# The sums of two weight quarters: GpSimd or VectorE, in an encoder layer with Winograd-like products

## The chip, the cores and the metric

The kernel runs on one core of one Trainium2 chip. The metric is the device time of one execution in microseconds (us); the time before is the median of three runs.

## The reference

One encoder layer on two token sets, 1024 prompt and 512 sample tokens, width 2048, all in fp32. In short:

```
h = rms_norm(x, pre_g);  z = h @ w_in            # 2048 -> 5632 columns
q, k, v, g_attn, u, vg, g_gmlp = split(z)
a = window_attention(rope(q), rope(k), v, sink) * silu(g_attn)
m = spatial_gating(gelu(u), gelu(vg), ln_g, ln_b, ws, bs) * silu(g_gmlp)
y = concatenate([a, m]) @ w_out
x = x + rms_norm(y, post_g)
x = x + sigmoid(x @ w_pg) * (p @ w_pe)
```

The three big products (w_in, w_out, w_pg) are where the change lies.

## The kernel before

**Products.** Each of the big products is cut into 2x2 blocks: two halves of the 1536 tokens (768 each), two halves of the inner dimension (1024 each), and the weight columns in pairs of 128. A pair is computed with seven block products instead of eight, in the manner of Strassen and Winograd: tables A_OF and B_OF (lines 48 to 51) name, for each of the seven, one operand quarter or the sum or difference of two (sign 0, 1 or -1), and one weight quarter or the sum or difference of two. In both tables five of the seven have a sign other than 0. The sums of the products are made when they leave PSUM (leave_product, line 250).

**Sweeps, segments, passes.** There are five sweeps (line 786): a, b and c for w_in, y for w_out, p for w_pg, with 8, 6, 8, 8 and 8 pairs. A sweep runs the seven products in the order 3, 5, 7, 1, 4, 2, 6 (line 46); one product over all pairs of a sweep is a segment, one product of one pair a pass. A pass is 48 matmuls: eight slices k of the inner dimension, two groups of 384 tokens, and three matmuls each, as every operand and weight is split in a high and a low part (mm3, lines 170 to 174).

**Operands and weights.** The operand of a segment, eight tiles of 128x768, is loaded by fetch_operand (line 230), summed on VectorE where the table says so, and split by split_operand (line 244): ScalarE copies the tile into the high part (line 163), VectorE subtracts to get the low part (line 165). There are eight buffers for split operands, so tile k of the next segment can be split only when the last pass of this one has used tile k. The weights of a pass, one tile of 128x1024, are made by make_weights (line 212): it issues the loads of one or two quarters on SyncE, then sums two quarters on GpSimd where the sign isn't 0 (line 223, through add or sub at lines 152 and 155), then splits the sum like an operand (line 227). Raw weight tiles (pool wrp) have four buffers, split ones (wtp) three. The raw tiles stand in the profile as wra, wrb, wrc, wry, wrp by sweep, the split ones as wta to wtp, the operands as ara and aa and so on.

**Order of the work.** The order of each engine's instructions is the order in which the program emits them, and that is planned by the class Line (line 54): every piece of work is a generator, and the number that it yields is the time in us after which its next part is due, on a clock that advances by 0.1733 us a matmul. So the weight job for pass j + 3 is started 1.5 us into pass j (line 873), its sum is due 9.0 us after its loads, its split 3.5 us after the sum, once pass j has been emitted (line 225); the split's subtraction comes 1.2 us behind its copy.

**Beside the products** run the embedding product p @ w_pe at the start (its results leave PSUM by VectorE copies, line 385), the norms, rope (lines 471 to 483, with two steps on GpSimd), the attention and the gating blocks. GpSimd also adds the squares of x for the norm (line 322) and the last sum of the output (line 556).

Of the kernel before, what the change touches and what calls it, by code (L numbers as in the profile page):

```python
# [90 lines left out]
def when(done):  # L91
    while not done():
        yield 0.5
# [3 lines left out]
def tile_encoder_layer(ctx: ExitStack, tc: tile.TileContext, xT, pT, wall, pre_g, post_g, sink,  # L97
# [62 lines left out]
    V, G = nc.vector, nc.gpsimd  # L160

    def split_to(src, hi, lo, us=1.2):
        nc.scalar.activation(hi, src, AF.Copy)  # L163
        yield us
        sub(V, lo, src, hi.bitcast(F32))
# [27 lines left out]
    def load_w(dst, f, h):  # L193

        if f[0] == "c":
            load(dst, wall[f[1], :, h * 1024:(h + 1) * 1024])
            return
        for i in range(2):
            src = wall[f[1] + 2 * h + i].rearrange("p (k n) -> p k n", k=4)
            load(dst[:, i * 512:(i + 1) * 512].rearrange("p (k n) -> p k n", k=4),  # L200
                 src[:, :, f[2]:f[2] + P])
# [10 lines left out]
    def make_weights(j, sw, pr, i):  # L212

        nm = f"{sw.name}{pr}_{i}"
        sign, *quarters = B_OF[pr]
        rs = []
        for kh, n in quarters:
            r = wrp.tile([P, 1024], F32, tag="wr", name=f"wr{nm}_{n}{kh}")
            load_w(r, sw.pairs[i][n][0], kh)
            rs.append(r)  # L220
        yield 9.0
        if sign:
            (add if sign > 0 else sub)(G, rs[0], rs[0], rs[1])
            yield 3.5
        yield from when(lambda: passes[0] >= j - 2)
        w = wtp.tile([P, 2, 1024], F32R, tag="wt", name=f"wt{nm}")
        yield from split_to(rs[0], w[:, 0, :], w[:, 1, :])
        weights[j] = w
# [174 lines left out]
    def embed():  # L403
        for j in range(16):
            line.until(lambda: j // 4 in wpe)
            if j in (1, 6):
                line.spawn(pe_weights(2 + j // 4))
            if j == 8:
                line.spawn(load_late())
            if j == 12:  # L410
                line.spawn(make_weights(1, *items[1]))
            w = wpe[j // 4]
            for h in range(2):
                line.until(lambda: (0, h) in pq and (1, h) in pq)
                ps = banks(f"pspe{j}_{h}")
                for k in range(2):
                    a = (j % 4) * 256 + k * P
                    for c in range(2):
                        mm3(ps[:, c, 0:CH], [w[:, s, a:a + P] for s in range(2)],
                            [pq[k, h][:, s, c * CH:(c + 1) * CH] for s in range(2)], k == 0, k == 1, 0.1733)  # L420
                    line.run_due()
                line.spawn(leave_pe(j, h, ps), 0.1)
# [435 lines left out]
    made_along = {(0, k) for k in range(8)} | {(2, k) for k in range(8)} | {(S_P, k) for k in range(8)}  # L858

    line.spawn(make_weights(0, *items[0]), 34.0)  # L860
    line.spawn(x0_normed(), 25.0)
    embed()
    pq.clear()
    embedded.append(True)
    line.spawn(make_weights(2, *items[2]))

    j = 0
# [99 lines left out]
```

## Time and profile before

| | |
|---|---|
| median of three runs | 2611.05 us (2610.92 to 2614.11) |
| the profiled execution | 2611.79 us |
| its span, first to last instruction | 2610.0 us |
| mean granted TensorE clock | 0.983 |
| busy: PE, DVE, ACT, POOL | 2503.3, 1703.8, 958.4, 736.8 us |
| DMA | 645.97 MB, mean 248 GB/s |

PE is TensorE, DVE VectorE, ACT ScalarE, POOL GpSimd, SP SyncE. A row of the profile names a group of instructions by line, engine, operation and tiles (out<-in, buffer numbers left out); "<-" followed by an engine names what ended a wait. A line such as L152 is that of the helper add, so it is shared by many tiles. Matmuls overlap, so PE counts as busy when it is merely slow; the number of matmuls in a stretch (x290) tells its pace. A DVE instruction is recorded to its end and the next one may start 0.08 us before that.

### The profile page before, as it was taken

Reading aid. Unit: us, or ns where it says so; the run is one execution under the profiler, and the core shown is the slowest. Engines: PE = TensorE matmul, PEld = TensorE weight load, DVE = VectorE, ACT = ScalarE, POOL = GpSimd, SP = SyncE. Lnnn points to the kernel's source line nnn. Section 1 sums busy time; section 2 is a strip of 40 time slices with the busy share of each in tenths; the row PEclk is TensorE's granted clock in tenths of the full one; section 3 lists DMA queues with packets and bytes.
Section 4 is the critical chain, followed back from the end, with each engine's and each line's share of the span. In section 5 each row is a group of like instructions: output and inputs, shape, how many; then the busy total and the mean of one; then the engine's idle time right before and its main releaser. Section 6 shows DMA issues by size and latency. Waiting matters only on the chain.

```text
span 2610.0 us, 36511 instructions
## 1 busy us (share of the span) xinstructions
PE 2503.3 (96%) x14268; PEld 2462.0 (94%) x14268; DVE 1703.8 (65%) x1883; ACT 958.4 (37%) x1378; POOL 736.8 (28%) x316
## 2 busy tenths in 40 slices
PE   5998999999999999999999999999999999999998
PEld 5998999999989999999999999999999999999998
DVE  3657566766667757777767665465566876666773
ACT  3142222323675543333546732332232223322321
POOL 4164324355012202302222013112310321433434
PEclk8999999999999999999999999999999999999999
DMA  6967776666575679879656677566577987879885
GB/s 228 360 237 239 259 248 218 202 206 235 181 263 183 186 245 298 308 252 308 211 173 223 215 269 256 211 224 222 171 233 253 332 302 287 284 246 318 306 301 204
DMA packets 372109, 645.97 MB, mean 248 GB/s; under 512 B 29280, under 2 KB 211680, under 8 KB 371936
## 3 DMA queue, kind: packets, MB, share of 16 engines
q1 hardware_dynamic: 371936, 643.63, 72.7%
q8 instruction: 112, 1.84, 0.3%
q14 instruction: 61, 0.50, 0.1%
HBM read 533.43 MB, written 110.10 MB: 247 GB/s over the span
## 4 chain that ended last, share of the span: by engine, by line
PE 71%; DVE 12%; ACT 5%; issue 5%; POOL 3%; DMA 3%; SPq 0%; POOLq 0%; DVEq 0%; ACTq 0%
PE psy L172 5%; PE psy L173 5%; PE psy L171 5%; PE psp L172 5%; PE psc L173 5%; PE psc L172 5%; PE psp L173 5%; PE psc L171 5%; PE psp L171 5%; PE psa L172 4%; PE psa L171 4%; PE psa L173 4%; PE psb L172 3%; PE psb L173 3%; PE psb L171 3%
## 5 line engine op out<-in xcount | busy, mean ns | idle before, releaser
L171 PE MATMUL psa<-aa,wta 128*128 128x384 f32 x896 | 304.8, 340 | 9.0 <-DVE oa L152 5.2
L172 PE MATMUL psa<-aa,wta 128*128 128x384 f32 x896 | 304.2, 339 | 3.2 <-DVE aa L155 3.2
L171 PE MATMUL psy<-ay,wty 128*128 128x384 f32 x896 | 303.1, 338 | 4.1 <-ACT ay L163 4.1
L171 PE MATMUL psc<-ac,wtc 128*128 128x384 f32 x896 | 305.9, 341 | 1.0 <-ACT ac L163 1.0
L172 PE MATMUL psp<-ap,wtp 128*128 128x384 f32 x896 | 301.6, 337 | 4.6 <-DVE ap L155 4.6
L172 PE MATMUL psy<-ay,wty 128*128 128x384 f32 x896 | 303.1, 338 | 2.2 <-DVE ay L155 2.2
L171 PE MATMUL psp<-ap,wtp 128*128 128x384 f32 x896 | 301.5, 337 | 3.8 <-ACT ap L163 3.8
L172 PE MATMUL psc<-ac,wtc 128*128 128x384 f32 x896 | 301.5, 337 | 1.7 <-DVE ac L155 1.7
L173 PE MATMUL psa<-aa,wta 128*128 128x384 f32 x896 | 303.0, 338 | 0.0
L173 PE MATMUL psy<-ay,wty 128*128 128x384 f32 x896 | 302.3, 337 | 0.0
L173 PE MATMUL psc<-ac,wtc 128*128 128x384 f32 x896 | 301.4, 336 | 0.0
L173 PE MATMUL psp<-ap,wtp 128*128 128x384 f32 x896 | 300.8, 336 | 0.0
L171 PE MATMUL psb<-ab,wtb 128*128 128x384 f32 x672 | 230.7, 343 | 0.5 <-DVE ua L152 0.5
L172 PE MATMUL psb<-ab,wtb 128*128 128x384 f32 x672 | 226.2, 337 | 2.5 <-DVE ab L155 2.5
L173 PE MATMUL psb<-ab,wtb 128*128 128x384 f32 x672 | 225.9, 336 | 0.0
L171 PEld LDWEIGHTS psa<-aa,wta 128*128 128x128 f32 x896 | 170.9, 191 | 10.7 <-issue 4.8
L172 PEld LDWEIGHTS psa<-aa,wta 128*128 128x128 f32 x896 | 170.9, 191 | 5.6 <-DVE aa L155 5.4
L172 PEld LDWEIGHTS psp<-ap,wtp 128*128 128x128 f32 x896 | 169.3, 189 | 6.7 <-DVE ap L155 6.4
L171 PEld LDWEIGHTS psy<-ay,wty 128*128 128x128 f32 x896 | 170.6, 190 | 4.9 <-ACT ay L163 4.8
L172 PEld LDWEIGHTS psy<-ay,wty 128*128 128x128 f32 x896 | 170.5, 190 | 4.1 <-DVE ay L155 3.8
L171 PEld LDWEIGHTS psp<-ap,wtp 128*128 128x128 f32 x896 | 169.3, 189 | 4.9 <-ACT ap L163 4.7
L172 PEld LDWEIGHTS psc<-ac,wtc 128*128 128x128 f32 x896 | 169.5, 189 | 2.5 <-DVE ac L155 1.9
(254 smaller groups left out, 5432.3 us busy)
## 6 DMA issues: line engine op xcount, KB each, us to landing
wrc<-wall SPq DMA_DIRECT2D x96, 512.0 KB, 7.0
arb<-h SPq DMA_DIRECT2D x96, 384.0 KB, 6.1
arc<-h SPq DMA_DIRECT2D x96, 384.0 KB, 5.5
wry<-wall SPq DMA_DIRECT2D x72, 512.0 KB, 6.0
wrp<-wall SPq DMA_DIRECT2D x72, 512.0 KB, 7.2
arp<-x SPq DMA_DIRECT2D x88, 384.0 KB, 5.8
wra<-wall SPq DMA_DIRECT2D x60, 512.0 KB, 5.7
ara<-h SPq DMA_DIRECT2D x80, 384.0 KB, 5.4
```

The source lines that it names most:

```text
L171: nc.tensor.matmul(ps, lhsT=l[0], rhs=r[0], start=start, stop=False)
L172: nc.tensor.matmul(ps, lhsT=l[0], rhs=r[1], start=False, stop=False)
L173: nc.tensor.matmul(ps, lhsT=l[1], rhs=r[0], start=False, stop=stop)
```

## The change

The sums and differences of two weight quarters go to VectorE instead of GpSimd, and the planner's wait behind such a sum is 1.6 us instead of 3.5. Nothing else is changed.

```diff
@@ -220,8 +220,8 @@
             rs.append(r)
         yield 9.0
         if sign:
-            (add if sign > 0 else sub)(G, rs[0], rs[0], rs[1])
-            yield 3.5
+            (add if sign > 0 else sub)(V, rs[0], rs[0], rs[1])
+            yield 1.6
         yield from when(lambda: passes[0] >= j - 2)
         w = wtp.tile([P, 2, 1024], F32R, tag="wt", name=f"wt{nm}")
         yield from split_to(rs[0], w[:, 0, :], w[:, 1, :])
```

## Rows read from the trace of the kernel before

**Rows 1.** The page, busy us of each engine (share of the span) xinstructions.

```profile
PE 2503.3 (96%) x14268; PEld 2462.0 (94%) x14268; DVE 1703.8 (65%) x1883; ACT 958.4 (37%) x1378; POOL 736.8 (28%) x316
```

**Rows 2.** Waits of PE, whole span: for whom, us in total, times, longest.

```profile
PE pspe L171 <- ACT pa L163: 11.7, 1, 11.7
PE ss_x L291 <- POOL accx L152: 11.6, 2, 10.4
...
PE s L172 <- DVE ks L155: 8.6, 8, 2.1
PE t L652 <- ACT p L645: 5.4, 19, 1.6
...
PE psa L171 <- DVE oa L152: 5.2, 2, 4.5
...
PE psa L171 <- ACT aa L163: 2.6, 2, 2.4
...
PE psb L171 <- DVE ua L152: 0.5, 1, 0.5
```

**Rows 3.** Stretches of 50 us: length, busy (xinstructions) by engine, PEclk, DMA share, GB/s.

```profile
core 0: us, PE busy (x) PEld busy (x) DVE busy (x) ACT busy (x) POOL busy (x), PEclk, DMA share, GB/s
250.00:300.00 50.00, 43.64 (x234) 42.31 (x234) 36.24 (x27) 17.03 (x20) 26.21 (x10) 0.93 0.83 278
...
1650.00:1700.00 50.00, 50.00 (x290) 50.00 (x290) 21.89 (x21) 17.06 (x21) 5.89 (x2) 1.00 0.40 144
...
2250.00:2300.00 50.00, 46.33 (x263) 45.11 (x262) 33.87 (x28) 14.38 (x17) 22.17 (x9) 1.00 0.81 277
2500.00:2550.00 50.00, 46.12 (x256) 45.16 (x255) 37.80 (x32) 15.43 (x18) 24.96 (x10) 0.97 0.80 269
```

**Rows 4.** Timeline of DVE, then POOL, then PE, 2249 to 2265 us.

```profile
2250.25 2.92 DVE L155 TENSOR_TENSOR arp<-arp,arp 128x768 f32<-128x768 f32 x1
...
2254.83 7.41 DVE L155 TENSOR_TENSOR ap<-arp,ap 128x768 fp32r<-128x768 f32 x4
2262.17 1.21 DVE L155 TENSOR_TENSOR wtp<-wrp,wtp 128x1024 fp32r<-128x1024 f32 x1
2263.30 1.81 DVE L155 TENSOR_TENSOR ap<-arp,ap 128x768 fp32r<-128x768 f32 x2
...
2249.95 2.41 POOL L152 TENSOR_TENSOR wrp<-wrp,wrp 128x1024 f32<-128x1024 f32 x1 [2.36 <-DMA wrp<-wall]
2254.99 2.51 POOL L152 TENSOR_TENSOR op<-op,lxpg 128x768 f32<-128x768 f32 x1 [2.64 <-DVE op L158]
2258.70 2.73 POOL L152 TENSOR_TENSOR wrp<-wrp,wrp 128x1024 f32<-128x1024 f32 x1 [1.20 <-DMA wrp<-wall]
...
2262.30 0.44 PE L172 MATMUL psp<-ap,wtp 128*128 128x384 f32 x1 [1.15 <-DVE ap L155]
...
2264.30 0.45 PE L172 MATMUL psp<-ap,wtp 128*128 128x384 f32 x1 [0.69 <-DVE ap L155]
```

**Rows 5.** POOL's groups, whole span: busy us, mean ns, idle before and its ends.

```profile
L152 POOL TENSOR_TENSOR wrc<-wrc,wrc 128x1024 f32<-128x1024 f32 x24 | 60.6, 2525 | 265.8 <-DMA wrc<-wall 140.1 <-DVE wtc L155 88.3 <-DMA ma<-oc 9.7
```

**Rows 6.** DVE on tile wtc: duration ns min/median/max, first and last start.

```profile
L155 DVE TENSOR_TENSOR wtc<-wrc,wtc x56: 1209/1224/3429, 1057.3 to 1599.5; 128x1024 fp32r<-128x1024 f32 x56
```

**Rows 7.** DVE's groups in sweep c, by shape, the last one out of PSUM.

```profile
L155 DVE TENSOR_TENSOR wtc<-wrc,wtc 128x1024 fp32r<-128x1024 f32 x56 | 82.2, 1468 | 6.7 <-ACT wtc L163 6.6
...
L155 DVE TENSOR_TENSOR ac<-arc,ac 128x768 fp32r<-128x768 f32 x56 | 59.1, 1076 | 2.3 <-ACT ac L163 2.2
...
L152 DVE TENSOR_TENSOR arc<-arc,arc 128x768 f32<-128x768 f32 x24 | 28.4, 1184 | 1.7 <-DMA arc<-h 1.7
...
L152 DVE TENSOR_TENSOR vc<-vc,psc 128x768 f32<-128x768 f32 x16 | 15.2, 951 | 34.9 <-PE psc L173 34.9
```

**Rows 8.** Timeline: DVE at 101 us, POOL at 104 and at 2554 us.

```profile
101.12 0.96 DVE L385 COPY pe<-pspe 128x768 f32<-128x768 f32 x1 [1.12 <-PE pspe L173]
...
103.94 2.40 POOL L155 TENSOR_TENSOR wra<-wra,wra 128x1024 f32<-128x1024 f32 x1 [29.94 <-DMA wra<-wall]
...
2554.30 2.81 POOL L152 TENSOR_TENSOR wrp<-wrp,wrp 128x1024 f32<-128x1024 f32 x1 [4.26 <-DMA wrp<-wall]
```

**Rows 9.** Timeline of ACT at 256 us.

```profile
256.24 1.06 ACT L163 ACTIVATE wta<-wra 128x1024 fp32r<-128x1024 f32 x1 [16.75 <-POOL wra L152]
```

## The prediction

> **What bounds the kernel now.** Read the busy line first [rows 1]: TensorE (PE) is busy for 2503.3 of 2610.0 us, so nothing can be won that does not remove some of its 106.7 idle us, or of the time it runs at a lower clock. The profiled execution took 2611.79 us (span 2610.0 and 1.79 around it), 0.74 us above the median of 2611.05.
>
> Next, who PE waits for [rows 2]. Two kinds of wait must be kept apart. Waits such as those for ACT pa and POOL accx (11.7 and 11.6 us) belong to the start and to the norms; they hang on other work than the changed adds. The second kind are waits for one of the operand tiles aa, ab, ac, ay, ap (the ScalarE copy or the VectorE subtraction that splits it in two) or, in and just after sweep a, for a tile that a product is left in: the view has twelve such rows, from 5.2 us (DVE oa) down to 0.5 us (DVE ua), together 32.6 us. A weight tile (wta to wtp) stands in no row: weights are always split in time.
>
> Where are these waits? A stretch of 50 us without any holds 290 matmuls, one per 0.172 us; three stretches with a change of segment hold 234, 263 and 256 [rows 3]. They lack 56 + 27 + 34 = 117 matmuls, 20.2 us. Part of that is clock: in two of the three the granted clock averages 0.93 and 0.97, so around such a stall TensorE ran a while at the lower of its two levels (1.2 instead of 2.4 GHz); (0.07 + 0.03) x 50 = 5 us of the 20.2.
>
> Why the operand is late shows in one change of segment [rows 4]. VectorE works without a gap from 2250.25 us on, yet an add that needs 0.95 us takes 2.92, and four splits take 7.41 us instead of 4 x 0.87. Each long one lies under a GpSimd instruction: the weight adds at 2249.95 and 2258.70 and the final add of the output at 2254.99. PE waits for splits at 2262.30 and 2264.30, 1.15 + 0.69 = 1.84 us.
>
> **How dear the two engines' adds are.** GpSimd takes 2.53 us for a weight add, mean of 24 in sweep c [rows 5]. There are five sweeps with 38 pairs in all, and five of the seven products of each add two quarters: 190 adds. On VectorE the subtraction of the same shape, 128x1024 with both inputs in SBUF, is the nearest row: 1.21 us at best, 1.22 in the median [rows 6], and the next instruction starts 1.13 us after it [rows 4]. No row shows the add itself on VectorE; the bounds are 1.13 and, if a GpSimd instruction lies over it, 3.43 us, the longest of these subtractions. I take 1.13, since few GpSimd instructions will be left.
>
> **What VectorE gets back.** In sweep c GpSimd does hardly anything but weight adds. There the weight splits average 1468 ns against a median of 1224 [rows 6, 7]. The operand splits take 1076 ns and the operand adds 1184, against 951 for an operation of their size with one input in PSUM, which loses nothing [rows 7]. That makes 56 x 0.24 + 56 x 0.125 + 24 x 0.23 = 26 us lost over the sweep's 40 adds, 0.66 us each. So on the average VectorE gains less than it pays: 190 x (1.13 - 0.66) = 89 us more work, from 65% to about 69% of the span. Nowhere does that make it the bound by itself. But at a change of segment every operation is back to back and has two SBUF inputs, and there an add costs about 2.0 us (2.92 - 0.95 in [rows 4]; 7.41 - 4 x 0.87 = 3.9 for one weight add and one output add). There the exchange is 2.0 against 1.13.
>
> The Trainium skill (SBUF — State Buffer, Who interferes with whom) says that GpSimd and a VectorE operation with two SBUF inputs take a shared port pair in turns, for a whole instruction. Taken so for every add, VectorE would become emptier, not fuller. The rows agree where VectorE has such an operation ready (2.92 us for 0.95), and not on the average. The sum goes by the rows.
>
> **The sum.**
> - Changes of segment. In the order of emission the second weight add of [rows 4] comes after the operand add that follows the last product, so VectorE has just one add in front of the splits for which PE waits at 2262.30 and 2264.30, while GpSimd ran both as soon as their quarters landed. 2 x 2.0 - 1.13 = 2.9 us less lateness there, more than the 1.84 us of PE waiting; the splits behind the second add gain nothing by it. I take half of all such waits: 32.6 / 2 = -16. Bounds: none, and all 32.6.
> - Clock. Half of the stalls gone should save about half of the 5 us seen in [rows 3], and as much in the changes of segment not shown: -4. Bounds 0 and -8.
> - Attention. PE waits for ks, the transposed p and others for 8.6 + 5.4 = 14 us [rows 2]; some sit behind blocked VectorE work, most are plain latency: -2. Bounds +3 and -5.
> - The wait that VectorE inherits. The add now waits for the landing of its two quarters in VectorE's queue, and evacuations of PSUM and splits stand behind it. Lining up the planner's order of emission with the trace, 174 of the 190 adds had both quarters landed when VectorE ended the operation emitted before; 16 would have waited, 23.7 us in all. In only five would the next operation start later than it did, by 5.3 us together. The first is the worst: at 103.78 the quarter lands, and the copy of 101.12 and the one after it stand behind it [rows 8]. That stops the embedding for nearly 3 us, but just after it PE waited 2.4 us (the longest of the ACT aa waits, [rows 2]) for an operand that hung on the same add. The last of the sixteen is that of 2554.30 [rows 8], which would hold the next operation back by 0.25 us. I charge +3; bounds 0 and 23.7.
> - Quiet changes of segment, where GpSimd's add hid beside VectorE operations that read PSUM, now have 1.13 us in front of the splits: +3, bounds 0 and +10.
> - ScalarE. Its weight copy is emitted 1.9 us earlier in the plan (1.6 instead of 3.5 after the add). In sweep a it once waited 16.75 us for GpSimd, whose add stood behind the rope's product, with an evacuation that PE needed behind it [rows 9]. This now waits for VectorE's queue; the gain is inside the first item. Freed buffers and SyncE: the second quarter's buffer is freed by VectorE instead, somewhat later, the first quarter's by the split, earlier: 0.
> - GpSimd's other work (x squares, rope, output adds) starts earlier; nobody critical waits for it but the x norm, whose last square comes from ScalarE: 0.
>
> Sum -16 - 4 - 2 + 3 + 3 = -16; 2611.79 - 16 = 2595.8 for the profiled execution, 0.74 less for a median: about 2595 us, 0.6% faster.
>
> **Rivals.**
> 1. *VectorE's queue waits for DMA* (slower). For it: GpSimd waited for a landing before most of its adds (in sweep c 140.1 us before 24 of them, [rows 5]), and an in-order VectorE must not do the same. Against: GpSimd got there early, VectorE late, as the count above says. Price: if all 23.7 us reach PE and the shorter blocking gives back only 10, 2611 + 14 = 2625. It decides from the point where more wait reaches PE than the 16 + 4 us of relief. Chance 0.13.
> 2. *Fuller VectorE eats the relief* (no change). Its 89 us of added work fall into the passes before and after each change of segment and push splits back by what was won: 2611 within 5. Against: [rows 4], where two blocks of 2 us give way to one add. Chance 0.15.
> 3. *All operand waits go*, with their clock loss: 2611 - 32.6 - 8 - 2 = 2568; against it, waits for ScalarE remain. Chance 0.1.
> That the add isn't what blocks VectorE can hardly be, with [rows 6] showing 1.2 to 3.4 us for one shape.
>
> **Numbers.** My forecast has the remaining 0.62. Faster by over 0.2% (5 us, about what a measurement can tell from no change): forecast and third rival, 0.72; same 0.15; slower 0.13. The range leaves out most of rival 3 and the upper half of rival 1: 2580 to 2616.
>
> **What would show it.** GpSimd down by about 480 us to some 240; VectorE's weight splits near 1.23 us on the average; 190 adds of about 1.2 us on VectorE; PE's waits for operand tiles at about half of 32.6 us; a granted clock nearer to 1.00 in the stretches of [rows 3]. Wrong if VectorE shows long waits for weight landings, or if operand waits stay and VectorE is busy without gap before them though its operations have their short durations.

## The result and the profile after

| | before | after |
|---|---|---|
| median | 2612.58 us (4 runs, 2610.92 to 2615.35) | 2573.34 us (4 runs, 2570.40 to 2576.83) |
| ratio, 95% interval | | 0.9853, 0.9838 to 0.9867 |
| the profiled execution | 2611.79 us | 2570.40 us |
| its span | 2610.0 us | 2568.6 us |
| mean granted TensorE clock | 0.983 | 0.989 |

The kernel became 39 us faster, in the forecast direction and by 2.4 times the 16 us forecast; 2573 lies below the range. The busy line of the page and PE's waits after the change, to be laid beside [rows 1, 2]:

```profile
PE 2486.1 (97%) x14268; PEld 2453.0 (95%) x14268; DVE 1759.9 (69%) x2073; ACT 964.9 (38%) x1378; POOL 256.3 (10%) x126
```

```profile
PE pspe L171 <- ACT pa L163: 11.8, 1, 11.8
PE ss_x L291 <- POOL accx L152: 11.5, 2, 10.3
...
PE pspe L171 <- DVE pe L385: 8.4, 7, 3.2
PE s L172 <- DVE ks L155: 8.0, 8, 2.1
PE psa L171 <- DVE oa L152: 4.2, 2, 3.5
...
PE psp L171 <- ACT ap L163: 2.5, 3, 1.6
PE t L652 <- ACT p L645: 2.1, 12, 0.2
PE tnvg L492 <- ACT va L529: 2.1, 1, 2.1
PE psp L172 <- DVE ap L155: 1.9, 3, 0.7
PE psa L172 <- DVE aa L155: 1.8, 2, 1.3
PE psy L171 <- ACT ay L163: 1.7, 1, 1.7
PE psy L172 <- DVE ay L155: 1.6, 1, 1.6
...
PE psc L172 <- DVE ac L155: 0.6, 1, 0.6
...
PE psa L171 <- ACT aa L163: 0.2, 1, 0.2
```

Of the same waits in the kernel before, these rows are needed beside those of [rows 2]:

```profile
PE pspe L171 <- DVE pe L385: 5.3, 6, 3.0
...
PE psp L172 <- DVE ap L155: 4.6, 6, 1.2
PE psy L171 <- ACT ay L163: 4.1, 2, 2.7
PE psp L171 <- ACT ap L163: 3.8, 3, 2.2
PE tnvg L492 <- ACT va L529: 3.5, 1, 3.5
PE psa L172 <- DVE aa L155: 3.2, 6, 1.4
...
PE tnvg L492 <- ACT oa L529: 1.9, 1, 1.9
...
PE tnvg L492 <- ACT vb L529: 1.1, 1, 1.1
```

The busy line divides the 41.4 us between the two spans. The same 14268 matmuls are there. PE's idle time fell from 106.7 to 2568.6 - 2486.1 = 82.5 us, by 24.2; its busy time fell by 17.2 us though it did the same work, most of it by a higher clock, as shown further down. In the view of waits the rows of operand tiles and of tiles that a product is left in come to 14.5 us, where twelve came to 32.6: 18.1 us less. The attention's two rows (ks and p) went from 14.0 to 10.1. One row rose by more than 0.1 us: the embedding's wait for its PSUM copies, from 5.3 to 8.4.

The stretches with a change of segment that answer to [rows 3]; the same work comes 35 us earlier at the second and 38 to 40 us earlier at the third, so these two answer to 2250 and 2500 us:

```profile
250.00:300.00 50.00, 45.23 (x245) 44.54 (x245) 37.22 (x36) 16.48 (x19) 5.17 (x2) 0.93 0.81 275
2215.00:2265.00 50.00, 48.68 (x280) 48.10 (x279) 35.16 (x34) 14.29 (x17) 5.15 (x2) 1.00 0.81 280
2460.00:2510.00 50.00, 47.79 (x275) 47.22 (x274) 41.15 (x38) 16.23 (x19) 14.47 (x6) 1.00 0.83 281
```

234, 263 and 256 matmuls became 245, 280 and 275 of the 290 that fit. VectorE is a little busier in all three and PE less held up.

The same change of segment as in [rows 4], timeline of VectorE, then GpSimd, then PE:

```profile
2215.07 0.95 DVE L155 TENSOR_TENSOR arp<-arp,arp 128x768 f32<-128x768 f32 x1
2215.94 1.22 DVE L152 TENSOR_TENSOR wrp<-wrp,wrp 128x1024 f32<-128x1024 f32 x1
...
2218.81 3.48 DVE L155 TENSOR_TENSOR ap<-arp,ap 128x768 fp32r<-128x768 f32 x2
2222.21 1.21 DVE L155 TENSOR_TENSOR wtp<-wrp,wtp 128x1024 fp32r<-128x1024 f32 x1
2223.34 3.55 DVE L155 TENSOR_TENSOR ap<-arp,ap 128x768 fp32r<-128x768 f32 x4
...
2227.68 0.94 DVE L155 TENSOR_TENSOR arp<-arp,arp 128x768 f32<-128x768 f32 x1
2228.55 1.21 DVE L152 TENSOR_TENSOR wrp<-wrp,wrp 128x1024 f32<-128x1024 f32 x1
...
2219.03 2.44 POOL L152 TENSOR_TENSOR op<-op,lxpg 128x768 f32<-128x768 f32 x1 [7.39 <-DVE op L158]
...
2229.56 0.44 PE L171 MATMUL psp<-ap,wtp 128*128 128x384 f32 x1 [0.64 <-ACT ap L163]
2230.68 0.44 PE L172 MATMUL psp<-ap,wtp 128*128 128x384 f32 x1 [0.68 <-DVE ap L155]
```

The operand add of 2.92 us takes 0.95. One weight sum of 1.22 us stands in front of the splits and the second only behind the next operand add, as worked out from the order of emission. One long operation is left among these lines, the pair of splits of 3.48 us under the output's add on GpSimd. The two PE waits of [rows 4], 1.84 us, are gone; those behind the second sum remain, at 0.64 and 0.68 us where the kernel before has 1.29 and 0.55.

VectorE in sweep c (1048.6 to 1595 us, so that a few instructions of the sweep fall outside), by shape, beside [rows 7], and its waits for weight landings:

```profile
L155 DVE TENSOR_TENSOR wtc<-wrc,wtc 128x1024 fp32r<-128x1024 f32 x54 | 65.9, 1221 | 14.7 <-ACT wtc L163 14.6
L155 DVE TENSOR_TENSOR ac<-arc,ac 128x768 fp32r<-128x768 f32 x51 | 47.2, 949 | 1.8 <-ACT ac L163 1.7
L152 DVE TENSOR_TENSOR wrc<-wrc,wrc 128x1024 f32<-128x1024 f32 x24 | 29.2, 1218 | 0.8 <-DMA wrc<-wall 0.8
L152 DVE TENSOR_TENSOR arc<-arc,arc 128x768 f32<-128x768 f32 x24 | 22.8, 951 | 1.6 <-DMA arc<-h 1.6
```

```profile
DVE wra L155 <- DMA wra<-wall: 8.9, 5, 4.2
...
DVE wrp L152 <- DMA wrp<-wall: 5.1, 3, 3.1
```

In sweep c every shape is at its shortest time: 1221 for 1468 ns, 949 for 1076, 951 for 1184. In sweeps a and p, where GpSimd keeps other adds, the weight splits still average 1447 and 1552 ns (1515 and 1481 before). The waits for landings are seven rows, 22.6 us in 19 waits. Over the kernel VectorE's busy time rose by 56.1 us, while 190 sums came in whose starts take 1.13 us each, 215 us; so it got back some 159 us, 0.83 us a sum.

### The profile page after: what moved, and what is told of

Same layout as the page of the kernel before. It is cut to its first block, busy times and chain, and to the rows that moved or that the text cites. A ratio compares the mean times of both kernels' runs of the same rounds, so it can differ in the third digit from the quotient of the medians.

```text
span 2568.6 us, 36268 instructions
## 1 busy us (share of the span) xinstructions
PE 2486.1 (97%) x14268; PEld 2453.0 (95%) x14268; DVE 1759.9 (69%) x2073; ACT 964.9 (38%) x1378; POOL 256.3 (10%) x126
## 3 DMA queue, kind: packets, MB, share of 16 engines
q8 instruction: 112, 1.84, 0.3%
## 4 chain that ended last, share of the span: by engine, by line
PE 76%; DVE 9%; DMA 4%; issue 4%; ACT 3%; POOL 2%; SPq 1%; POOLq 0%; DVEq 0%; ACTq 0%
PE psy L172 6%; PE psy L171 6%; PE psy L173 5%; PE psc L172 5%; PE psc L171 5%; PE psc L173 5%; PE psa L172 5%; PE psa L173 5%; PE psa L171 5%; PE psp L172 4%; PE psp L173 4%; PE psp L171 4%; PE psb L173 4%; PE psb L171 4%; PE psb L172 4%
```

## The experiments

Each edit is shown against the changed kernel. All ratios are to the kernel before, on the same chip, with 95% intervals. Where two experiments are set against each other, their medians come from different chips; on these the kernel before took 2610.89 to 2613.05 us.

### The engine alone, the plan alone

```diff
             (add if sign > 0 else sub)(V, rs[0], rs[0], rs[1])
-            yield 1.6
+            yield 3.5
```

> The sum is on VectorE, the planner's wait behind it stays 3.5 us. Theory (the sums on GpSimd hold up VectorE operations with two SBUF inputs at the changes of segment, and with them PE): nearly all of the gain comes from the engine, 2570 to 2582 us. Rival (a good part comes from the split being emitted 1.9 us earlier, which frees ScalarE's queue): 2588 to 2602 us.

```diff
-            (add if sign > 0 else sub)(V, rs[0], rs[0], rs[1])
+            (add if sign > 0 else sub)(G, rs[0], rs[0], rs[1])
             yield 1.6
```

> The sum stays on GpSimd, the planner's wait behind it is 1.6 us. Theory: no gain, 2606 to 2620 us, rather slower since ScalarE comes earlier to a copy that waits for GpSimd. Rival (order of emission): 2590 to 2600 us.

Measured: the engine alone 2573.18 us, ratio 0.9851 (0.9837 to 0.9864), the whole gain; the plan alone 2618.03 us, ratio 1.0022 (1.0011 to 1.0033), a little slower. The 1.6 in place of 3.5 is worth nothing here.

### Some of the sums only

```diff
+            near = i in (1, 2)
-            (add if sign > 0 else sub)(V, rs[0], rs[0], rs[1])
-            yield 1.6
+            (add if sign > 0 else sub)(V if near else G, rs[0], rs[0], rs[1])
+            yield 1.6 if near else 3.5
```

> Only the sums for the passes 1 and 2 of each segment are on VectorE (wait 1.6 us): these are due around the change of segment. They are 50 of the 190. Theory (PE loses its time at the changes of segment): more than half of the gain of 39 us, 2583 to 2592 us. Rival (every moved sum gains alike, by shorter chains or a freer VectorE): 50/190 of 39 us = 10 us, 2600 to 2605 us.

```diff
+            near = i in (1, 2)
-            (add if sign > 0 else sub)(V, rs[0], rs[0], rs[1])
-            yield 1.6
+            (add if sign > 0 else sub)(G if near else V, rs[0], rs[0], rs[1])
+            yield 3.5 if near else 1.6
```

> The complement: the 140 sums of the other passes on VectorE, those of passes 1 and 2 on GpSimd as before. Theory: less than half of the gain, 2594 to 2606 us. Rival: 140/190 of 39 us = 29 us, 2580 to 2587 us.

Measured: 2590.15 us with the 50 sums moved, ratio 0.9918 (0.9904 to 0.9931), 21.7 us below the 2611.87 of its kernel before; 2589.22 us with the other 140, ratio 0.9916 (0.9902 to 0.9931), 22.6 us. The first is as the theory had it, the second is better than the theory's 2594 and short of the rival's 2587. A sum around a change of segment is worth 0.43 us, one elsewhere 0.16. So half of the gain comes from a quarter of the sums, but not nearly all of it: the blocked VectorE cost PE time in other places too. PE's waits show where. With the 50 sums moved, the rows of operand tiles and of tiles that a product is left in fall from 32.6 to 19.0 us, the attention's rows (s, t and o) stay at 17.2 where they were 16.5, and tnvg goes from 6.5 to 5.0. With the other 140 they come to 24.7, 12.5 and 3.8. The two gains add up to 44 us; their intervals reach some 3.5 us either way, so that this is not clear of the 39 of both together.

### Blocking without anyone waiting for the sum

```diff
             (add if sign > 0 else sub)(V, rs[0], rs[0], rs[1])
+            add(G, rs[1], rs[1], rs[1])
             yield 1.6
```

> The changed kernel, and behind each sum on VectorE GpSimd adds the spent second quarter to itself: same size, two inputs in SBUF, nobody reads the result, but its buffer is held some 2.5 us longer. Theory (what costs time is that a GpSimd add holds up VectorE operations with two SBUF inputs, and not that something waits for GpSimd's result): the gain goes and VectorE has its own sums besides, 2605 to 2640 us, short stops of 2 to 3 us in VectorE's operations again. Rival (the long chain load, GpSimd sum, ScalarE copy): 2570 to 2582 us.

```diff
             (add if sign > 0 else sub)(V, rs[0], rs[0], rs[1])
+            for _ in range(2):
+                G.memset(rs[1], 0.0)
             yield 1.6
```

> As the kernel with the idle GpSimd adds (2623 us), but in place of each idle add GpSimd fills the spent quarter with zeros, twice: it writes the same tile for about as long, holds its buffer alike, and reads nothing. Theory (it is GpSimd's reading that holds up VectorE operations with two SBUF inputs): no long VectorE operations from it, 2570 to 2582 us. Rival (what the idle adds cost is the spent quarter's buffer, which SyncE waits for): 2600 us or more.

Measured: with idle GpSimd adds 2623.46 us, ratio 1.0046 (1.0030 to 1.0062): the gain is gone and 10 us more. With idle GpSimd writes 2568.45 us, ratio 0.9848 (0.9832 to 0.9864): the whole gain is kept, and the time is a little below the 2570 expected. GpSimd's group of sweep y and SyncE's wait for it, first with idle adds, then with idle writes:

```profile
L152 POOL TENSOR_TENSOR wry<-wry 128x1024 f32<-128x1024 f32 x40 | 94.5, 2363 | 362.4 <-DVE wry L152 257.1 <-DVE wry L155 73.1 <-DMA wry<-wall 15.8
```

```profile
SPq L140 <- POOL wry L152: 116.0, 35, 8.1
```

```profile
L225 POOL MEMSET wry<- 128x1024 f32 x80 | 76.5, 957 | 373.2 <-DVE wry L152 236.7 <-DVE wry L155 81.1 <-issue 31.7
```

```profile
SPq L140 <- POOL wry L225: 113.6, 28, 7.5
```

Two writes of 957 ns hold the quarter nearly as long as an add of 2363, and SyncE waits as long for its buffer, 113.6 against 116.0 us; that is not it. What differs is VectorE. Its weight splits of sweep y with idle adds, then with idle writes (ns, min/median/max):

```profile
L155 DVE TENSOR_TENSOR wty<-wry,wty x56: 1207/1226/2573, 1612.7 to 2095.4; 128x1024 fp32r<-128x1024 f32 x56
```

```profile
L155 DVE TENSOR_TENSOR wty<-wry,wty x56: 1215/1224/1228, 1578.6 to 2053.0; 128x1024 fp32r<-128x1024 f32 x56
```

With the adds some splits take up to 2573 ns, their mean is 1607; with the writes none is over 1228. (In sweeps a and p, where GpSimd has other adds, the longest splits are 2872 and 2591 ns with the writes too; the changed kernel has 2907 and 2746.) Nothing waits for either's result, so no chain through GpSimd is needed to explain the loss. That agrees with what the Trainium skill (SBUF — State Buffer, Who interferes with whom) says: a VectorE instruction with two SBUF inputs contends with a GpSimd instruction that reads SBUF, not with one that only writes it.

### What the sums still cost on VectorE

```diff
-            (add if sign > 0 else sub)(V, rs[0], rs[0], rs[1])
             yield 1.6
```

> The 190 sums are left out altogether; both quarters are loaded and the first alone is split. Theory: VectorE's own sums cost little, since 1.13 us fit in where 2 us did not: 2560 to 2571 us. Rival (VectorE, 69% busy, now sets the changes of segment): 15 us or more below the changed kernel, under 2558 us.

```diff
-        yield 9.0
+        yield 12.0 if sign else 9.0
```

> The changed kernel with the sum due 12 instead of 9 us after its loads, so that its quarters have landed when VectorE comes to it. In the changed kernel VectorE waited 22.7 us for landings before 19 sums, and leaving the sums out gave 26.5 us. Theory (the waits mostly meet slack; what the sums cost is their 1.13 us in the changes of segment and in attention): 2567 to 2577 us, of which up to 3 us from the start. Rival (the waits for landing are what VectorE's sums cost): 2552 to 2562 us.

Measured: without the sums 2546.82 us, ratio 0.9750 (0.9731 to 0.9769); with the sums later 2574.57 us, ratio 0.9859 (0.9843 to 0.9876). The first expectation failed, on the rival's side. The sums cost 2613.05 - 2546.82 = 66 us on GpSimd and still 2573.34 - 2546.82 = 26.5 us on VectorE: it is not free there, it is cheaper. The second kept to its theory: the landings are not the 10 to 20 us of its rival. VectorE's waits for quarters before its sums fall from 22.6 to 5.8 us and the embedding's row from 8.4 to 6.0, but nothing is won in all. It is not a clean test, though: PE now waits 4.3 us for a weight tile (wta, rows of 3.3 and 1.0), which it never did in the changed kernel, so a gain of a few us may be hidden. Most of the 26.5 us is then the work of the sums in VectorE's queue or ScalarE's waits for them, which leaving them out takes away together, so that the two are not told apart; without the sums the operand rows of PE's waits come to 7.4 us instead of 14.5. Which of VectorE's later operations pass the cost on was not followed further.

### The rest of GpSimd's work

```diff
-            add(G, o, o, x[:, 0:HT])
+            add(V, o, o, x[:, 0:HT])
...
-            mul(G, o[:, s:e], o[:, s:e], c)
+            mul(V, o[:, s:e], o[:, s:e], c)
...
-        add(G, o, o, b)
+        add(V, o, o, b)
...
-        yield from accumulate(x_acc[0], k == 0, t, None if k == 0 else work(f"sq{k}"), G)
+        yield from accumulate(x_acc[0], k == 0, t, None if k == 0 else work(f"sq{k}"), V)
...
-        yield from accumulate(x_acc[1], k == 0, t, t, G)
+        yield from accumulate(x_acc[1], k == 0, t, t, V)
```

The planner's waits behind them become 1.5 (output), 3.2 and 1.5 us (rope).

> The changed kernel with GpSimd's other adds and products moved to VectorE as well: squares of x (31 adds), rope's product and sum, the last add of the output (32). Theory: the blocking that is left goes too (waits for oa, aa and ap, about 12 us with clock), and the chain of 15 squares at the start runs at 0.95 instead of 1.84 us an add, for which PE waits 10 us: 2548 to 2563 us. Rival (VectorE, at over 75%, becomes late): 2570 to 2590 us.

Only the two lines of the squares:

> The changed kernel with only the squares of x moved to VectorE. Theory: the start loses up to 10 us of PE's wait for accx and VectorE is no longer blocked around 165 to 187 us: 2558 to 2567 us. Rival (loads or ScalarE's squares set that wait): 2569 to 2576 us.

All of it, with the weight sums due later as above:

> The kernel with all of GpSimd's adds and products on VectorE (2543.8 us), the weight sums due 12 instead of 9 us after their loads. Theory: 2538 to 2544 us, the stop of the embedding near 95 us shorter. Rival (later sums make splits or weights late in a fuller VectorE): 2546 us or more.

Measured: all 2543.77 us, ratio 0.9738 (0.9719 to 0.9757), below the 2548 to 2563 expected and faster than both kernels; the squares alone 2560.57 us, ratio 0.9811 (0.9790 to 0.9833), as expected: PE's wait for accx, 11.5 us, is gone, and the embedding's row rises from 8.4 to 12.0. All with later sums took 2546.20 us, ratio 0.9752 (0.9737 to 0.9766), on the rival's side of that expectation and no better than without; PE waits for wta there too, 3.9 us. The busy line of the fastest:

```profile
PE 2477.9 (98%) x14268; PEld 2445.9 (96%) x14268; DVE 1782.9 (70%) x2185; ACT 965.1 (38%) x1378; POOL 12.6 (0%) x14
```

GpSimd falls to 12.6 us. VectorE takes over what was 244 us of GpSimd's time and is only 23 us busier than after the change; its longest weight split is 1228 ns in every sweep, so nothing lengthens them any more. The rival had it at over 75% and late.

## Why the prediction was wrong

**Right: the cause and the place.** PE's rows for operand tiles were to lose half of 32.6 us, 16; they lost 18.1. The half was a choice and not worked out, so that the closeness is partly luck. In [rows 4] the order of the two sums, the 0.95 us in place of 2.92, and the two PE waits that vanish came out as worked out. That a GpSimd add over VectorE's operations is what costs is borne out by the kernels with idle adds and idle writes, one 50 us slower than the changed kernel, the other not.

**Right: the inherited waits, as to their number.** 16 waits and 23.7 us were counted from the trace of before, 19 and 22.6 came; the sixteen are not listed, so they can't be matched one by one. The first is the longest of the 19: VectorE waits 4.22 us at the start, with the copies of [rows 8] behind it, and the embedding's row rises by 3.1 us, which is the +3 charged; PE's wait for aa behind it falls from 2.6 to 0.2, as the prediction has it. A price of the later ones is not seen, but the kernel with later sums leaves a few us open.

The sum allowed 12 us of idle time and 4 of clock. The profiled execution gave 24.2 and 17.2, so that both fell short.

**Wrong: the clock.** The first step that failed is "Half of the stalls gone should save about half of the 5 us seen in [rows 3], and as much in the changes of segment not shown: -4". PE's busy time, the same matmuls, fell by 17.2 us. The clock records of the two traces put 88.3 us at the lower level before and 60.7 after; at half the pace that is at most 44 and 30 us lost, so 14 of the 17.2 are clock. The term was read from 5 us in three stretches and took as much again for the rest. The trace of before has seven stretches at the lower level whose longest wait ahead is one for such a tile (operand, or left by a product); they are 30.7 us long, so 15 us lost. Five of them, 20.5 us, have no counterpart after the change: 10 us back where 4 were counted on. Two more, 6.8 us, stood behind a wait of tnvg and one of the attention and are gone too; these the term did not have.

One change of segment in the kernel before, as stretches ahead of, in and behind the time at the lower level (columns as in [rows 3]):

```profile
1755.00:1760.00 5.00, 5.00 (x31) 5.00 (x30) 5.00 (x6) 1.26 (x2) 1.34 (x1) 1.00 0.48 166
...
1765.70:1769.10 3.40, 3.17 (x10) 3.17 (x11) 3.35 (x5) 1.17 (x2) 0.00 (x0) 0.50 0.97 315
1769.20:1775.00 5.80, 5.80 (x35) 5.80 (x35) 1.70 (x2) 0.00 (x0) 1.82 (x1) 1.00 1.00 372
```

and what PE did ahead of it, in the timeline of the same kernel:

```profile
1762.34 0.44 PE L172 MATMUL psy<-ay,wty 128*128 128x384 f32 x1 [0.54 <-DVE ay L155]
...
1764.94 0.44 PE L171 MATMUL psy<-ay,wty 128*128 128x384 f32 x1 [1.47 <-ACT ay L163]
...
1765.93 0.69 PE L172 MATMUL psy<-ay,wty 128*128 128x384 f32 x1 [0.55 <-DVE ay L155]
```

PE waited 0.54 and 1.47 us, and from 1765.7 on the granted clock is 0.50, 1.2 GHz: ten matmuls in 3.4 us, where twice as many fit. After the change PE does not stop at this change of segment, and the two stretches of 50 us from 1700 to 1800 us hold 289 and 290 matmuls at a clock of 1.00.

"Half of the stalls gone should save about half" takes the loss for a share of the stall, and the traces do not bear that out. At 260 us the wait for oa fell from 4.5 to 3.5 us, and the whole stretch behind it stayed at the lower level, first before, then after:

```profile
260.50:267.20 6.70, 5.00 (x15) 4.63 (x16) 6.70 (x6) 6.53 (x9) 3.52 (x2) 0.50 0.98 343
```

```profile
260.50:267.20 6.70, 5.33 (x16) 4.96 (x17) 6.70 (x8) 6.69 (x9) 0.00 (x0) 0.50 1.01 350
```

Behind a wait for accy that took 5.1 us in both kernels, the time at the lower level fell from 10.2 to 6.8 us; and after the change there is a new one of 3.4 us behind a wait for ks of 2.1. So no rule for a single stall comes out of these traces.

How large the clock's part is in the median is less sure than in this pair of profiles. The 42 runs of the kernel before made beside the experiments have a mean granted clock of 0.981 to 0.987, on the average 0.9844; the four of the changed kernel 0.989, 0.986, 0.988 and 0.986, and the profiled one is the fastest of them. By these averages 41 us were lost before and 33 after, 8 us less: still twice the forecast, and just at its bound. Across the profiled experiments the clock rises roughly as PE's idle time falls: 0.983 at 110.2 us in the kernel with the plan alone changed, 0.984 at 118.6 with idle adds, 0.986 and 0.985 at 96.5 and 92.1 with part of the sums moved, 0.989 at 82.5 after the change, 0.990 at 68.1 without sums, 0.993 at 63.0 with all on VectorE.

**Wrong by about as much: the idle time.** 24.2 us against 12 (16 + 2 less the two charges of 3). The charge of +3 for quiet changes of segment does not show in any row. The attention's rows gave 4.6 instead of 2 (ks and p 3.9, pt 0.7). And the transposes of vg (tnvg), which the sum put at nothing, went from 6.5 us of PE's waits to 2.1. With the 2.1 us more from the operand rows these make up the difference. The kernel with the 140 other sums moved says the same: the waits of attention and tnvg fall by 6.7 us there, with the 50 sums by only 0.8. The prediction looked for the relief at the changes of segment alone and had 2 us for the rest.

**Too low, with no effect on the time that shows: what VectorE gets back.** 0.66 us a sum was an average over three groups of sweep c; by the busy time, which rose by 56 us and not 89, it was 0.83. The kernel without sums gives the whole price more directly: VectorE is busy for 1517.1 us there, so that GpSimd's sums lengthened its work before by 1703.8 - 1517.1 = 187 us, 0.98 us each.

**The rivals.** The third, that all operand waits go with their clock loss, gave 2568 and a chance of 0.1: near in its time, but 14.5 us of those waits remained; tnvg, the attention and the clock made up for it. The first, VectorE's queue waiting for landings, had the waits and not their price. The second fell with the busy line: VectorE is fuller and PE faster.

ScalarE's queue does not explain the gain: its copies of weights wait longer for the sums than before, 414 us in all against 265, in part in place of waits for PE. The two largest of these rows after the change are shown; they had 80.5 us in 8 waits and 47.9 in 10 when GpSimd made the sums. The wait of [rows 9], 16.75 us, became the 14.8 of the first:

```profile
ACT wta L163 <- DVE wra L152: 112.3, 17, 14.8
ACT wtp L163 <- DVE wrp L152: 78.9, 20, 7.7
```

## What to carry to other kernels

Price a GpSimd instruction that reads SBUF by what it does to VectorE's operations with two SBUF inputs, not by its own time: here sums on an engine with 72% of its time free cost 66 us, and 26.5 on one that was more than twice as busy. Look for that price at every place where PE waits behind VectorE, and not only where VectorE works without a gap: here half of the gain came from sums that were not due at a change of segment. Where PE stalls, take the clock loss from the whole run, stretch by stretch, and not as a share of the stall; it also differs from run to run. When a helper is moved to an in-order engine, lining up the order of emission with the landings in the old trace can tell about how often it will wait: here 16 waits were counted and 19 measured.

## What the runs showed of the hardware

GpSimd filling a tile in SBUF, 957 ns for 128x1024, leaves VectorE's weight splits alone (1228 ns at most in sweep y), while GpSimd adds of the same tile make some of them up to 2573 ns long. And the clock was a good part of the gain: 14 of 41 us in the two profiled executions, and some 8 of 39 by the average clock of all runs.
